# The end of a layer norm by TensorE, split first casts, and four order tables in a two-layer decoder trunk

## The chip, the cores and the metric

The kernel runs on one core of a Trainium2 chip. The metric is the device time of one execution in microseconds. Three runs of the kernel before took 552.74, 552.90 and 553.92 us; the median is 552.90.

## The reference

A trunk of two layers works on 256 tokens of width 1024. Each layer has a token mixer, a cross-attention into 256 memory tokens and a SwiGLU feed-forward block of width 2816. The residual is scaled by ALPHA and followed by a layer norm:

```python
x = layer_norm(ALPHA * x + sub, ln_mix_g[i], ln_mix_b[i])
x = layer_norm(ALPHA * x + swiglu(x, w_ffn_in[i], w_ffn_out[i]), ln_ffn_g[i], ln_ffn_b[i])
```

The mixer of layer 0 is a gated spatial mixer: u, v and the memory queries come from one projection of x, v is normalised and mixed over the positions of a 128-token chunk, and the result is multiplied by u. The mixer of layer 1 is causal attention with 12 heads. Everything is float32. What leaves the kernel is the layer norm behind the second feed-forward block: for each row, (r - mean) * g * rs + b, where rs is the reciprocal square root of variance plus epsilon.

## The kernel before

**Precision.** A float32 operand is kept as two parts that TensorE multiplies at its fast float32 rate: a high part, a rounded copy made by ScalarE (`nc.scalar.copy` in `split`, L379), and a low part, the difference, made by VectorE (L380). A product of two such operands takes three passes: high by high, low by high and high by low. Operands that aren't split (float32 on both sides) are multiplied as true float32, which the trace shows as two matmul instructions for each product.

**Weights.** All weights lie in one array in the order of use and are loaded in units of 128 x 2048 through a ring of four buffers (`Stream`, L194 to L290). SyncE's queue (SP) issues most loads, GpSimd's queue (POOL) those that are added onto a block already loaded (L220).

**The first projection.** L426 to L448 project x onto v. The contraction of 1024 runs in eight steps of 128 rows, kk from 0 to 7. A step's load brings 256 columns of x transposed, followed by 768 columns of weights. Step 0 comes in three pieces (x; 384 weight columns by ScalarE's queue; 384 more), the others in one. The step's x is split into `xT` (L439, L440), its weights into `hl`, in two cuts of 384 for steps 0 and 1. Twelve products follow (L446): for each half h of the weight columns, high by high, x low by weight high, x high by weight low, for both 128-token tiles. Ahead of them, 37 small bfloat16 products (L415) keep TensorE busy until the first load has landed.

**The u projections.** They follow (L943 to L953) as six tiles of PSUM, written by 16 products each. Each tile is read out by ScalarE (L950) and VectorE (L951). They share four PSUM buffers, tag "mm", with the two query tiles ahead of them, which L475 to L477 read out.

**The end.** Tokens are two tiles of 128 rows, 0 and 1. `last_tile` (L892 to L905) closes tile 1 in three column pieces of 512, 384 and 128. For each piece TensorE makes 18 products, VectorE adds them to the residual (L903) and takes statistics (L499). `finish` (L502 to L514) then aggregates the statistics (L505), adds epsilon (L507), lets GpSimd raise the sum to the power -0.5 (L508, called the power below), and for the same three pieces subtracts the mean and multiplies by the gain (L511, the subtract), multiplies by rs and adds the bias (L512, the scale), and stores (L514): two pieces by SP, the last by ScalarE's queue.

**The order of the work.** TensorE's instructions run as the program writes them. For VectorE, ScalarE and SP the order is written out in tables: `VECTOR_ORDER`, `SCALAR_ORDER` and `SYNC_ORDER` list the engine's instructions, numbered as the program issues them, in the order in which they are to run, and `keep_order` (L358) binds each to the one ahead of it. An engine works strictly along its table, so an instruction that waits holds all that stand behind it. GpSimd's order is left to the scheduler.

Of the kernel before, what the change touches and what calls it, by code (L numbers as in the profile page):

```python
# [30 lines left out]
LAST_PIECES = ((0, 512), (512, 896), (896, 1024))  # L31
PASSES = ((0, 0), (0, 1), (1, 0))
# [161 lines left out]
class Stream:  # L194
# [128 lines left out]
)  # L323
SCALAR_ORDER = (
# [42 lines left out]
def build(nc, tc, ins, out):  # L367
    ET = mybir.EngineType
    with (
# [15 lines left out]
        def mm_tile(name):  # L385
            return ps.tile([P, 512], F32, tag="mm", name=name)
# [836 lines left out]
```

## Time and profile before

| What | Value |
|---|---|
| Runs, median (lowest to highest) | 552.90 us (552.74 to 553.92) |
| Profiled execution, its own time | 552.48 us |
| Its span, first to last instruction | 550.8 us |
| TensorE matmul busy | 542.6 us, 99% |
| VectorE busy | 501.5 us, 91% |
| ScalarE busy | 374.5 us, 68% |
| GpSimd busy | 47.7 us, 9% |
| First product of the projection | 5.31 us |
| Last product's result taken up | 543.85 us |
| Mean granted TensorE clock | 0.996 |

Rows of a timeline give the start, the duration, the engine, the line, the operation, the tile written and the tiles read, the shape and the count of instructions merged; in brackets stands the idle time ahead and what ended it. Rows of a table by stretches give, for each engine (PE, weight loads, VectorE, ScalarE, GpSimd), the busy time and the number of instructions, then the granted clock, the share of the 16 DMA engines and GB/s. PE is TensorE, DVE VectorE, ACT ScalarE, POOL GpSimd; a q behind a name is that engine's queue. Rows of groups give the count, the busy time and the mean ns of one. Rows of the chain of waits give start, length and the work.

### The profile page before, as it was taken

How to read it: one execution, taken by the hardware profiler on the slowest of the kernel's cores; microseconds unless marked ns; L12 is line 12 of the kernel's file. 1: busy time of each engine (PE TensorE's matmuls, PEld its weight loads, DVE VectorE, ACT ScalarE, POOL GpSimd, SP SyncE). 2: the span in 40 equal slices, each digit the busy share in tenths (PEclk: the TensorE clock that was granted, in tenths of full speed). 3: DMA queues.
4: the chain of work that ended last, by engine and by line, in shares of the span. 5: the costliest groups of instructions: out<-in, count | busy, mean ns of one | idle time of the engine just before them, and what ended most of it. 6: DMA issues, size and time to landing. Idle time of an engine off the chain costs nothing.

```text
span 550.8 us, 7698 instructions
## 1 busy us (share of the span) xinstructions
PE 542.6 (99%) x2835; PEld 460.6 (84%) x2835; DVE 501.5 (91%) x707; ACT 374.5 (68%) x574; POOL 47.7 (9%) x59
## 2 busy tenths in 40 slices
PE   9999999999999999999999999999999999999994
PEld 8988878888888888888898888788888888888884
DVE  5799978999999999999989688589999999999997
ACT  5868759785858677683565667668768676876720
POOL 1012001020202020100000000111202020201000
PEclk9999999999999999999999999999999999999998
DMA  8997668479796988878539234513597698897622
GB/s 303 384 398 265 223 259 221 154 131 328 155 343 132 300 220 229 275 271 273 198 137 397 105 130 161 114 77 153 97 360 133 249 266 271 233 255 220 218 69 77
DMA packets 23718, 120.97 MB, mean 220 GB/s; under 512 B 2688, under 2 KB 4736, under 8 KB 13824
## 3 DMA queue, kind: packets, MB, share of 16 engines
q1 hardware_dynamic: 17344, 99.16, 47.8%
q0 software_dynamic: 5760, 20.97, 21.4%
q8 instruction: 22, 0.36, 0.3%
q10 hardware_dynamic: 576, 0.34, 0.3%
q14 instruction: 16, 0.13, 0.1%
HBM read 119.42 MB, written 1.05 MB: 219 GB/s over the span
## 4 chain that ended last, share of the span: by engine, by line
PE 98%; DMA 1%; DVE 1%; DVEq 0%; ACT 0%; issue 0%
PE fof L404 11%; PE Xf L404 10%; PE Xg L404 10%; PE fog L404 9%; PE Zg L404 7%; PE Zf L404 7%; PE qk L404 6%; PE opc L404 4%; PE opa L404 4%; PE va L404 3%; PE bv L404 3%; PE pu L404 3%; PE pvm L404 3%; PE hkm L404 2%; PE hqm L404 2%; PE pg L404 2%
## 5 line engine op out<-in xcount | busy, mean ns | idle before, releaser
L379 ACT CAST spl_s_M<-raw_s_T 128x1024 fp32r<-128x1024 f32 x80 | 82.4, 1052 | 22.9 <-DVE raw_s_T L259 18.0
L380 DVE TENSOR_TENSOR spl_s_M<-raw_s_T,spl_s_M 128x1024 fp32r<-128x1024 f32 x80 | 95.6, 1217 | 2.4 <-ACT spl_s_M L379 2.1
L380 DVE TENSOR_TENSOR spl_s_M<-raw_s,spl_s_M 128x1024 fp32r<-128x1024 f32 x60 | 71.7, 1217 | 3.2 <-ACT spl_s_M L379 3.1
L379 ACT CAST spl_s_M<-raw_s 128x1024 fp32r<-128x1024 f32 x60 | 61.0, 1050 | 17.5 <-DMA raw_s<-in_w 13.3
L404 PE MATMUL fof<-spl_w,htf 128*128 128x512 f32 x264 | 63.0, 390 | 0.0
L404 PEld LDWEIGHTS fof<-spl_w,htf 128*128 128x128 f32 x264 | 49.3, 188 | 10.2
L404 PE MATMUL fog<-spl_w,htg 128*128 128x512 f32 x228 | 54.2, 390 | 0.0
L380 DVE TENSOR_TENSOR spl_w<-raw_w,spl_w 128x1024 fp32r<-128x1024 f32 x44 | 53.2, 1215 | 0.1
L404 PEld LDWEIGHTS fog<-spl_w,htg 128*128 128x128 f32 x228 | 42.7, 188 | 8.8
L259 DVE TENSOR_TENSOR raw_s_T<-raw_s_T,raw_s 128x1024 f32<-128x1024 f32 x40 | 48.4, 1217 | 0.1
L379 ACT CAST spl_w<-raw_w 128x1024 fp32r<-128x1024 f32 x44 | 45.7, 1055 | 1.0 <-PE fof L404 1.0
L404 PE MATMUL qk<-x2T,spl_qk 128*128 128x512 f32 x192 | 36.0, 343 | 0.0
L220 POOL DMA_DIRECT2D raw_s<-in_w x20 | 17.1, 856 | 217.1 <-DVE spl_s_M L380 201.4
L404 PEld LDWEIGHTS qk<-x2T,spl_qk 128*128 128x128 f32 x192 | 29.4, 188 | 4.4
L404 PE MATMUL Xg<-spl_s_M,SgM 128*128 128x512 f32 x120 | 29.4, 394 | 0.0
L404 PE MATMUL Xf<-spl_s_M,SfM 128*128 128x512 f32 x120 | 29.3, 393 | 0.0
L404 PE MATMUL Zg<-spl_s_M,SgM 128*128 128x512 f32 x120 | 28.9, 390 | 0.0
L404 PE MATMUL Xf<-spl_s_M,x1T 128*128 128x512 f32 x120 | 28.9, 390 | 0.0
L404 PE MATMUL Zf<-spl_s_M,SfM 128*128 128x512 f32 x120 | 28.8, 389 | 0.0
L404 PE MATMUL Xg<-spl_s_M,x3T 128*128 128x512 f32 x120 | 28.8, 389 | 0.0
L404 PEld LDWEIGHTS Zg<-spl_s_M,SgM 128*128 128x128 f32 x120 | 22.5, 188 | 4.8 <-DVE SgM L380 0.2
L404 PEld LDWEIGHTS Xg<-spl_s_M,x3T 128*128 128x128 f32 x120 | 22.5, 188 | 4.7
(265 smaller groups left out, 1068.8 us busy)
## 6 DMA issues: line engine op xcount, KB each, us to landing
raw_w<-in_w SPq DMA_DIRECT2D x22, 1024.0 KB, 6.6
raw_s<-in_w SPq DMA_DIRECT2D x20, 1024.0 KB, 7.1
raw_s_T<-in_w SPq DMA_DIRECT2D x10, 1024.0 KB, 7.0
raw_s_T<-in_w POOLq DMA_DIRECT2D x20, 512.0 KB, 8.6
raw_s<-in_w POOLq DMA_DIRECT2D x20, 512.0 KB, 5.5
raw_o<-in_w SPq DMA_DIRECT2D x8, 1024.0 KB, 6.4
raw_qk<-in_w SPq DMA_DIRECT2D x6, 1024.0 KB, 4.8
raw_v<-in_w SPq DMA_DIRECT2D x7, 512.0 KB, 8.1
```

Source lines behind the costliest of these rows:

```text
L220: self.nc.gpsimd.dma_start(self.raw[name][:, sl], self.unit_ap(other)[:, sl], accum_op=ALU.add)
L259: self.nc.vector.tensor_add(raw, raw, self.raw[used[1]][:, sl])
L379: nc.scalar.copy(hi, src)
L380: nc.vector.tensor_sub(lo, src, hi.bitcast(F32))
L404: nc.tensor.matmul(o, lhsT, rhs, start=start, stop=stop, skip_group_check=on)
```

## The change

- Both tiles are finished and stored in pieces of 512, 256 and 256 columns. The products of `last_tile` keep their three pieces.
- For tile 1, columns 768 to 1023 are scaled by TensorE. A PSUM tile first receives the identity times the bias, two true float32 products that need nothing of the statistics. ScalarE multiplies the identity by rs, which gives a diagonal matrix; TensorE adds the diagonal times the subtracted columns; ScalarE copies the sum to SBUF and its queue stores it. VectorE only makes the subtract of that piece.
- The first 384 weight columns of step 0 are cast by two engines, 192 columns by ScalarE and 192 by VectorE. Step 1's load is cut in two: x with 384 weight columns, and the other 384.
- All order tables are new, and `POOL_ORDER` is added. In the new `VECTOR_ORDER`, 2 and 3 are the cast and the low part of step 0's x, 4 the new copy of 192 columns, 5 and 6 the low parts of its two weight cuts, 7 the cast of step 1's x; 26 to 29 read out the two query tiles, 36 and 37 are the adds of L951 for the first two u tiles; 660 to 667 finish tile 0, 668 to 675 are tile 1's adds and statistics, 676 to 682 finish tile 1. In the new `SYNC_ORDER`, 2 and 3 are the two loads of step 1, 6 and 7 those of steps 4 and 5. In the new `SCALAR_ORDER`, 10 to 13 are the casts of steps 4 and 5, x ahead of weights; 535 is tile 0's last store, 536 the diagonal, 537 the copy, 538 the last store.

```diff
+STORE_PIECES = ((0, 512), (512, 768), (768, 1024))
...
 VECTOR_ORDER = (
-    0, 2, 3, 4, 5, 6, 7, 8, 9, 10, 11, 12, 13, 14, 16, 15, 18, 17, 19, 20, 22, 21, 23, 24, 34, 29, 33, 25, 32, 38, 37,
...
-    661, 666, 663, 670, 664, 662, 671, 672, 673, 674, 675, 681, 676, 679, 677, 682, 680, 678,
+    0, 2, 4, 3, 5, 7, 6, 8, 9, 10, 11, 12, 13, 15, 14, 16, 17, 19, 18, 20, 22, 21, 24, 23, 1, 25, 34, 35, 30, 32, 38,
+    39, 33, 26, 47, 27, 56, 46, 49, 42, 43, 31, 48, 28, 57, 60, 37, 50, 36, 62, 29, 58, 51, 59, 40, 96, 61, 64, 41,
...
+    648, 633, 650, 646, 634, 649, 652, 651, 643, 653, 640, 647, 654, 669, 656, 658, 657, 655, 660, 659, 662, 668, 661,
+    664, 666, 670, 665, 663, 671, 672, 673, 667, 674, 675, 676, 677, 678, 682, 679, 680, 681,
 )
 SCALAR_ORDER = (
-    2, 3, 4, 5, 6, 7, 8, 9, 11, 10, 13, 14, 12, 15, 16, 0, 17, 1, 18, 19, 26, 27, 22, 24, 25, 31, 20, 32, 23, 41, 21,
...
+    2, 3, 4, 5, 6, 7, 9, 8, 0, 12, 10, 11, 13, 16, 15, 14, 17, 1, 18, 19, 26, 41, 22, 27, 24, 25, 31, 32, 42, 20, 23,
...
+    522, 530, 531, 523, 527, 532, 533, 534, 536, 535, 537, 538,
+)
+POOL_ORDER = (
+    0, 1, 5, 4, 6, 7, 2, 10, 3, 8, 9, 11, 12, 14, 13, 15, 16, 17, 18, 19, 20, 22, 21, 23, 24, 25, 26, 27, 28, 29, 30,
+    34, 33, 31, 32, 35, 36, 37, 38, 39, 40, 42, 41, 43, 44, 45, 46, 47, 48, 49, 50, 51, 52, 53, 54,
 )
 SYNC_ORDER = (
-    0, 1, 2, 3, 4, 18, 5, 6, 7, 8, 10, 9, 11, 12, 13, 14, 15, 19, 20, 16, 17, 24, 22, 25, 21, 26, 27, 28, 29, 23, 31,
...
+    0, 1, 3, 2, 4, 5, 19, 7, 6, 9, 8, 10, 11, 12, 20, 13, 14, 21, 15, 22, 16, 18, 23, 17, 25, 24, 26, 27, 28, 29, 30,
...
-    mine = [i for i in nc.cur_bb.bb.instructions if i.engine == engine and not str(i.opcode).startswith("Tile")]
+    mine = [i for i in nc.cur_bb.bb.instructions if i.engine == engine and not str(i.opcode).startswith(("Tile", "RegisterMove"))]
...
-                if kk == 0:
-                    for q, c0, c1 in ((nc.sync, 0, T), (nc.scalar, T, T + 384), (nc.sync, T + 384, D)):
-                        q.dma_start(rk[:, c0:c1], src[:, c0:c1])
-                else:
-                    nc.sync.dma_start(rk, src)
+                loads = {0: ((nc.sync, 0, T), (nc.scalar, T, T + 384), (nc.sync, T + 384, D)),
+                         1: ((nc.sync, 0, T + 384), (nc.sync, T + 384, D))}.get(kk, ((nc.sync, 0, D),))
+                for q, c0, c1 in loads:
+                    q.dma_start(rk[:, c0:c1], src[:, c0:c1])
...
                 for c0, c1 in cuts:
+                    if kk == 0 and c0 == 0:
+                        nc.scalar.copy(hl[:, 0, :192], rk[:, T:T + 192])
+                        nc.vector.tensor_copy(hl[:, 0, 192:c1], rk[:, T + 192:T + c1])
+                        nc.vector.tensor_sub(hl[:, 1, :c1], rk[:, T:T + c1], hl[:, 0, :c1].bitcast(F32))
+                        continue
                     split(hl[:, 0, c0:c1], hl[:, 1, c0:c1], rk[:, T + c0:T + c1])
...
-                for i, (c0, c1) in enumerate(LAST_PIECES if store else PIECES):
+                o = None
+                if store and tt:
+                    o = mm_tile("end")[:, :256]
+                    nc.tensor.matmul(o, ident, gb[:, 1, 768:], start=True, stop=False)
+                for c0, c1 in (STORE_PIECES if store else PIECES):
                     sl = slice(c0, c1)
                     nc.vector.scalar_tensor_tensor(r[:, sl], r[:, sl], mv[:, 0:1], gb[:, 0, sl], ALU.subtract, ALU.mult)
-                    nc.vector.scalar_tensor_tensor(r[:, sl], r[:, sl], rs, gb[:, 1, sl], ALU.mult, ALU.add)
+                    if c0 == 768 and o is not None:
+                        diag = const.tile([P, P], F32, name="diag")
+                        nc.scalar.mul(diag, ident, rs)
+                        nc.tensor.matmul(o, diag, r[:, sl], start=False, stop=True)
+                        nc.scalar.copy(r[:, sl], o)
+                    else:
+                        nc.vector.scalar_tensor_tensor(r[:, sl], r[:, sl], rs, gb[:, 1, sl], ALU.mult, ALU.add)
                     if store:
-                        (nc.scalar if i == len(LAST_PIECES) - 1 else nc.sync).dma_start(out[tt * P:(tt + 1) * P, sl], r[:, sl])
+                        (nc.scalar if c0 == 768 else nc.sync).dma_start(out[tt * P:(tt + 1) * P, sl], r[:, sl])
...
+    keep_order(nc, tc, ET.Pool, POOL_ORDER)
```

103 rows, old and new, of tables (SCALAR_ORDER, SYNC_ORDER, VECTOR_ORDER) are left out of this document.

## The prediction

> **What bounds the kernel now.** I read the page's busy line and chain of waits first, then the table by stretches, then the timelines of both ends.
>
> ```profile
> PE 542.6 (99%) x2835; PEld 460.6 (84%) x2835; DVE 501.5 (91%) x707; ACT 374.5 (68%) x574; POOL 47.7 (9%) x59
> PE 98%; DMA 1%; DVE 1%; DVEq 0%; ACT 0%; issue 0%
> ```
>
> ```profile
> 5.31:22.83 17.52, 17.52 (x97) 17.52 (x98) 13.08 (x21) 12.64 (x19) 0.00 (x0) 1.00 1.02 403
> 22.83:543.85 521.02, 520.98 (x2703) 439.25 (x2701) 483.74 (x674) 359.97 (x554) 45.38 (x50) 1.00 0.69 216
> 543.85:550.80 6.95, 0.00 (x0) 0.00 (x0) 3.88 (x10) 0.00 (x0) 0.85 (x1) 0.65 0.27 99
> ```
>
> From 5.31 to 543.85 TensorE (first busy column) is never without work: 17.52 of 17.52, then 520.98 of 521.02 us. So the middle, where most of the new order tables lie, can give nothing; it can only lose, where a reordered VectorE or ScalarE operand comes too late. Gains can come only from the 5.31 us ahead of the first product and the 6.95 us behind the last. A delay inside the stretch is paid in full. The profiled execution took 552.48 us, 1.68 beyond its span; the median of the runs, 552.90, is 0.42 above it. My sum is a difference made on this execution; I add it to the median.
>
> **The start: first casts.** Steps are the eight 128-row slices kk of the first projection, counted from 0, with 12 products each. The view is the timeline of VectorE and ScalarE.
>
> ```profile
> 4.52 0.29 DVE L439 CAST x0T<-raw_v 128x256 fp32r<-128x256 f32 x1 [3.52 <-DMA raw_v<-in_w]
> 5.29 1.07 DVE L380 TENSOR_TENSOR spl_v<-raw_v,spl_v 128x384 fp32r<-128x384 f32 x2
> 7.17 0.29 DVE L439 CAST x0T<-raw_v 128x256 fp32r<-128x256 f32 x1 [0.80 <-DMA raw_v<-in_w]
> 4.75 1.03 ACT L379 CAST spl_v<-raw_v 128x384 fp32r<-128x384 f32 x2 [2.21 <-DMA raw_v<-in_w]
> 9.78 0.41 ACT L439 CAST x0T<-raw_v 128x256 fp32r<-128x256 f32 x1 [0.48 <-DMA raw_v<-in_w]
> 10.09 0.83 ACT L379 CAST spl_v<-raw_v 128x768 fp32r<-128x768 f32 x1
> 10.95 0.96 DVE L380 TENSOR_TENSOR spl_v<-raw_v,spl_v 128x768 fp32r<-128x768 f32 x1 [0.23 <-ACT spl_v L379]
> 13.22 0.84 ACT L379 CAST spl_v<-raw_v 128x768 fp32r<-128x768 f32 x1 [0.16 <-DMA raw_v<-in_w]
> ```
>
> The first product waits for ScalarE's 384-column cast (4.75 plus half of 1.03). At 0.41 for 256 columns and 0.51 for 384, 192 columns take about 0.35 (bounds 0.26, half, and 0.41), so it ends at 5.10. VectorE's own 192 columns fit behind its 0.29 us cast, from 4.75 to about 5.05. The product starts at 5.15, 0.16 earlier. The clock is worth a look here:
>
> ```profile
> 6.64:545.95 539.31, 537.17 (x2795) 455.44 (x2794) 497.76 (x699) 372.15 (x571) 46.06 (x51) 1.00 0.70 221
> 545.95:550.80 4.85, 0.00 (x0) 0.00 (x0) 1.88 (x4) 0.00 (x0) 0.17 (x1) 0.50 0.29 108
> ```
>
> ```profile
> 5.31 1.01 PE L404 MATMUL va<-spl_v,x0T 128*128 128x384 f32 x2
> 7.94 0.51 PE L404 MATMUL va<-spl_v,x0T 128*128 128x384 f32 x2
> 14.18 0.51 PE L404 MATMUL va<-spl_v,x0T 128*128 128x384 f32 x2
> ```
>
> Products 12 and 48 of this stage start at 7.94 and 14.18, so one takes 0.173 us. The first two take 1.01 where a later pair takes 0.51: half speed. The trace's record of the granted clock begins, at 1.00, at 6.64. So work that moves ahead of 6.64 runs at half speed, and 0.16 us earlier is 0.08 to 0.16 gained; I take 0.10.
>
> That gain meets two places of the new order. **First**, VECTOR_ORDER now has "7, 6": the cast of step 1's x (7) ahead of step 0's second low part (6). The cast waits for step 1's load, here until 7.17, and the new loads put that piece last (SYNC_ORDER "3, 2"), so it lands no sooner with the same bytes ahead. Instruction 6, one half of the 1.07 us pair (0.55), would run from about 7.38 to 7.93. Queued behind it for TensorE is product 11, due at 7.76 before and 7.66 now; it starts at 7.98, and I add 0.08 for the restart (an estimate: half of the 0.16 by which a pair's 0.51 exceeds two times 0.173). TensorE is then 0.30 behind. **Second**, step 5 is loaded ahead of step 4 ("7, 6" in SYNC_ORDER), so step 4 lands where step 5 did, 13.22. ScalarE then needs 0.31 to its next start and 0.83, and VectorE another 0.96: the low part is there at 15.37. Product 53, the first to use it, was due at 15.04 (14.18 plus five times 0.173). TensorE is at least 0.36 behind. The two don't add: the later the stream is, the less the second costs. I take +0.36 (bounds -0.16, if step 1's piece lands by 6.8 and step 4 by 12.8, and +0.45). The extra load instruction costs SP 0.43 us; it is hidden, as the 16 engines are full in this stretch (share 1.02); uncovered it would cost those 0.43.
>
> GpSimd's table and the table of ScalarE move casts, loads and masks by places; POOL is 9% busy and I cost it at nothing, its cover being the other 91%; if that were gone, an accumulating load would be late by the power or mask put ahead of it, 0.4 to 1.4 us.
>
> **The end.** Again the row first, then the new order.
>
> ```profile
> 544.77 0.35 DVE L511 SCALAR_TENSOR_TENSOR xres<-xres,mvg,gb1ffn 128x128 f32<-128x128 f32 x1
> 545.04 0.15 DVE L507 TENSOR_SCALAR rsg<-mvg 128x1 f32<-128x1 f32 x1
> 545.11 1.27 DVE L511 SCALAR_TENSOR_TENSOR xres<-xres,mvg,gb1ffn 128x384 f32<-128x384 f32 x2
> 545.27 0.85 POOL L508 TENSOR_TENSOR rsg<-rsg,mhalf 128x1 f32<-128x1 f32 x1 [7.93 <-DVE rsg L507]
> 547.86 0.33 SPq L514 DMA_DIRECT2D out<-xres  x1
> ```
>
> The DMA issues of that stretch give KB each and us to landing:
>
> ```profile
> out<-xres SPq DMA_DIRECT2D x2, 256.0 KB, 2.2
> out<-xres SPq DMA_DIRECT2D x2, 192.0 KB, 1.9
> out<-xres ACTq DMA_DIRECT2D x2, 64.0 KB, 1.6
> ```
>
> The end is the last store: issued at 547.86, landed 2.0 later (its own share of the 2.2 median), at 549.87, and 0.93 more to the span's end. The new VectorE order is: epsilon directly behind the aggregate, then the 512-column subtract, the 256-column subtract (768 on), the 512-column scale, then subtract and scale of 512:768. Epsilon starts at 544.77, 0.27 earlier, and the power would start at 545.00. But the power takes as long as the VectorE instruction under way lets it: 0.56 us beside a 0.41 one, 1.42 beside a 1.23 one, each ending about 0.4 behind it:
>
> ```profile
> 91.03 0.41 DVE L470 TENSOR_TENSOR kkm<-hkm,kkm 128x256 fp32r<-128x256 f32 x1
> 91.21 0.56 POOL L522 TENSOR_TENSOR rsa<-rsa,mhalf 128x1 f32<-128x1 f32 x1 [3.93 <-DVE rsa L521]
> 363.57 1.23 DVE L380 TENSOR_TENSOR spl_s_M<-raw_s,spl_s_M 128x1024 fp32r<-128x1024 f32 x1
> 363.80 1.42 POOL L522 TENSOR_TENSOR rsc<-rsc,mhalf 128x1 f32<-128x1 f32 x1 [17.45 <-DVE rsc L521]
> ```
>
> Beside the 0.74 us subtract, from 544.84 to 545.58, it ends at 545.99, not at 545.56; before it ended at 546.12. So 0.27 earlier yields 0.13. VectorE's scale of 512 runs 546.02 to 546.77, the 256-column subtract (0.48, between 0.35 and 0.61) to 547.16, its scale from 547.20 to 547.68, the store is issued at 547.71. 128 KB should land in 1.75 (between 1.6 and 1.9): 549.46.
>
> The last quarter goes another way. ScalarE's diagonal waits for the power; behind it on ScalarE stand the first tile's last store, the copy and the last store. TensorE has only the second product behind that wait, VectorE's scale the last two instructions and both SP stores. Prices:
>
> ```profile
> L576 ACT ACTIVATE pb<-pb,mb 128x128 f32<-128x128 f32 x12 | 4.7, 395 | 6.5 <-DVE mb L567 6.5
> L950 ACT COPY uT<-pu 128x256 f32<-128x256 f32 x6 | 2.2, 369 | 2.3 <-PE pu L404 2.3
> 70.74 1.88 PE pvm L404 x16
> ```
>
> Diagonal 0.40 (0.30 to 0.47): 546.04 to 546.44. The product has true float32 operands; the nearest row has eight such products of 256 columns on half the array in 1.88 us, so 0.47 on all of it (bounds half of that and, at half clock, twice). Weights and the way until the result is out take 0.35, an estimate from the pair above (0.16 behind the second product, and about as much ahead): it ends at 547.31; copy until 547.71; store issued 547.74, landed 549.49. The bias product with the identity runs in TensorE's empty time at 543.8 and delays nobody. So the end is 549.49, 0.38 earlier. At half clock weights, product and copy end at 548.29, the store lands at 550.07: 0.20 later than before.
>
> Which clock? The record falls to 0.50 at 545.95, 2.1 us behind the last product. The identity product moves that by 0.43, and the diagonal's weights load at 546.49. As a fixed delay behind the last product that is even; but the identity product also fills the stretch ahead of the fall, 1.70 of 3.41 busy in place of 1.27 (second row below), so I take full speed, at two to one.
>
> ```profile
> 3.23:6.64 3.41, 3.29 (x23) 3.02 (x21) 1.79 (x4) 1.02 (x2) 0.00 (x0) 1.00 0.98 342
> 542.54:545.95 3.41, 1.27 (x12) 1.13 (x11) 3.15 (x10) 0.00 (x0) 0.68 (x1) 1.00 0.36 137
> ```
>
> The Trainium skill, page "TensorE: Matmul & The Clock Gate", section "Part 1: The HAM clock gate", has the clock decided by a window of 3.41 us that runs freely of the kernel. The trace agrees: rise and fall lie 539.31 apart, 158 windows of 3.413, the window before the rise was 3.29 busy and that before the fall 1.27. By that rule the phase differs between executions, and the diagonal runs fast in some and slow in others; the sum would be the two ends above by turns.
>
> One instruction is moved onto the path: the first tile's last scale (667) now stands ahead of the last tile's final add. Its cover is an idle stretch that the new order fills with the first tile's subtracts:
>
> ```profile
> 538.75 0.69 DVE L903 TENSOR_TENSOR xres<-xres,last 128x512 f32<-128x512 f32 x1 [0.67 <-PE last L404]
> ```
>
> I cost it at nothing; uncovered, 0.2 to 0.4.
>
> Sum: +0.36 - 0.38 = -0.02. Forecast 552.9.
>
> **Rivals.**
> - The start doesn't stall (-0.10), end as above: -0.48, 552.4. For it: a wait ends with a load's last part, and in another execution that may come 0.5 sooner; against it: both loads were waited for here (0.80 and 0.16 idle).
> - The diagonal meets the half clock: +0.36 + 0.20 = +0.56, 553.5.
> - Slower: a TensorE buffer in the u projections. Six tiles of 2.77 us each run from 28.38; the fourth (36.69) needs a PSUM tile that VectorE has read.
>
> ```profile
> 28.38 16.64 PE pu L404 x96
> 30.54 0.40 DVE L477 SCALAR_TENSOR_TENSOR qqm<-hqm,qqm 128x256 fp32r<-128x256 f32 x1
> ```
>
> Before, the second q tile was read out at 30.54. Now that read (29) stands behind two u splits, three memT splits, a km split and a 1.00 us normalisation; laying the rows behind one another in the new order (an estimate), the first buffer to come free is that of add 37, at 36.8. Each further 1.23 us split (the row at 363.57) that comes late there delays TensorE by as much, beyond the 0.36 that it is late anyway. From 1.1 us of such waiting on it decides: one split more gives 554.1, two 555.4. For it: VectorE is 91% busy; against it: the rows leave it just in time.
> - Faster: the first product catches a full clock at once. The half-clock stretch (5.31 to 6.64) is worth 0.67 at most: -1.15, 551.7.
>
> **How the numbers follow.** Chances: forecast 0.42, no stall 0.20, half clock 0.20, buffer 0.13, clock at the start 0.05. From the bounds: best start and end -0.16 - 0.5 (the end with the store of 64 KB's 1.6), so 552.2; worst +0.45 with the slow end, +0.20, and 667 uncovered, +0.3, so 553.9. That range leaves out the buffer and the early clock, 0.18. About 0.2% (1.1 us) is what a measurement of this kernel can tell from no change: faster 0.05 (the early clock), same 0.80, slower 0.15 (the buffer, and 0.02 for several bounds at once).
>
> **What would show it.** VectorE's low part of step 0 starting behind a cast near 7.2, with TensorE idle before product 11; a TensorE wait near 15; the power ending near 546.0 plus the stream's delay; the fp32 product with the diagonal taking 0.5 or 0.9. TensorE idle between 23 and 540 would make the forecast wrong, as would a first tile's last scale that holds the final add.

## The result and the profile after

The changed kernel takes 557.12 us (median of 8 runs, 555.79 to 560.07); the kernel before, beside it, 552.82 (552.27 to 553.92). The ratio is 1.0078, 95% interval 1.0064 to 1.0092: 4.3 us slower. The forecast was 552.9, the range 552.2 to 553.9. The spread has grown from 1.7 to 4.3 us, which is a finding of its own. The profiled execution took 556.10, 1.0 below the median, so its trace holds only 3.6 of the 4.3.

The first fence shows the busy line and the chain's shares, on the page of the changed kernel.

```profile
PE 544.5 (98%) x2839; PEld 459.8 (83%) x2839; DVE 501.7 (90%) x707; ACT 375.2 (68%) x576; POOL 48.0 (9%) x59
PE 81%; DVE 7%; issue 5%; DMA 4%; ACT 2%; POOL 1%; SPq 0%; POOLq 0%; ACTq 0%; DVEq 0%
```

Before, the chain was TensorE for 98%. Now 19% of it runs through other engines and loads: TensorE waits somewhere in the middle. The table by stretches says where. Columns: length, then busy time of TensorE, weight loads, VectorE, ScalarE, GpSimd, then clock, DMA share and GB/s. The first three rows are start, middle and end; the last three cut the middle into the first feed-forward block, the second layer's attention, and the second block.

```profile
5.04:22.70 17.66, 17.44 (x97) 16.81 (x98) 14.07 (x24) 13.52 (x21) 0.00 (x0) 1.00 1.03 401
22.70:547.04 524.34, 521.99 (x2704) 439.20 (x2703) 483.19 (x671) 359.23 (x552) 46.30 (x52) 1.00 0.68 214
547.04:554.40 7.36, 1.53 (x4) 0.42 (x3) 3.65 (x9) 0.77 (x2) 0.99 (x1) 0.69 0.25 90
76.00:270.00 194.00, 192.44 (x899) 160.16 (x897) 184.87 (x209) 137.29 (x182) 21.12 (x25) 1.00 0.76 228
270.00:400.00 130.00, 129.21 (x780) 110.61 (x779) 108.20 (x229) 89.36 (x185) 7.77 (x9) 1.00 0.47 154
400.00:547.00 147.00, 147.00 (x683) 122.79 (x682) 142.36 (x155) 94.37 (x115) 13.08 (x16) 1.00 0.73 218
```

Middle: 524.34 where it was 521.02, so +3.32 (idle time shows 2.35 of it; the ends of matmuls are modelled, and part of a wait is counted as busy). End: 7.36 where it was 6.95. The first projection ends 0.13 earlier, at 22.70, in an execution whose clock rose early (at 3.72; at 6.64 in the profile before). The largest stall lies in the first feed-forward block. The timeline around it:

```profile
139.87 1.05 ACT L384 CAST spl_s_M<-raw_s_T 128x1024 fp32r<-128x1024 f32 x1 [1.88 <-DMA raw_s_T<-in_w]
140.36 0.27 PE L849 MATMUL tpf<-ident,m1f 128*128 128x128 f32 x1
140.82 0.59 ACT L827 ACTIVATE sgf<-Xf 128x512 f32<-128x512 f32 x1
141.44 0.69 DVE L828 SCALAR_TENSOR_TENSOR m5f<-m5f,sgf 128x512 f32<-128x512 f32 x1 [2.02 <-ACT sgf L827]
142.19 0.33 PE L849 MATMUL tpf<-ident,m5f 128*128 128x128 f32 x1 [1.56 <-DVE m5f L828]
```

Read it upwards. TensorE waits for m5f, VectorE for sgf, and ScalarE stood at a cast that waited 1.88 for a load. In SCALAR_ORDER that cast (161) now stands ahead of sgf (149); before it stood behind. Two waits in the second layer's attention follow the same pattern, on the timeline of TensorE:

```profile
340.05 2.23 PE L409 MATMUL qk<-x2T,spl_qk 128*128 128x512 f32 x11 [0.24 <-ACT pT L1089]
...
354.65 1.20 PE L1087 MATMUL pt<-ident,pb 128*128 128x128 f32 x9 [0.40 <-DVE pb L601]
```

From start to start, beyond what such neighbours need elsewhere, the four largest stalls cost 1.73 (at 140), 0.41 (340), 0.57 (354) and 0.31 (385): 3.0 of the 3.32.

The end, on the timeline of the changed kernel:

```profile
547.97 0.15 DVE L516 TENSOR_SCALAR rsg<-mvg 128x1 f32<-128x1 f32 x1
548.20 0.99 POOL L517 TENSOR_TENSOR rsg<-rsg,mhalf 128x1 f32<-128x1 f32 x1 [5.71 <-DVE rsg L516]
549.22 0.40 ACT L527 ACTIVATE diag<-ident,rsg 128x128 f32<-128x128 f32 x1 [10.19 <-POOL rsg L517]
549.67 1.08 PE L528 MATMUL end<-xres,diag 128*128 128x256 f32 x2 [2.18 <-ACT diag L527]
550.79 0.37 ACT L529 COPY xres<-end 128x256 f32<-128x256 f32 x1 [1.17 <-PE end L528]
551.20 0.35 ACTq L533 DMA_DIRECT2D out<-xres  x1
```

Counted from the last tile's last add (547.04; 543.85 before), the power ends at 2.15 where 2.14 was predicted, the diagonal at 2.58 (2.59). The products take 1.08, and ScalarE's store, the last, is issued 4.16 after the add, where 3.89 was predicted.

That late store does not set the end here. SP's last store, issued 3.87 after the add, landed 6.00 after it. SP then goes through the signals of the other DMAs (their semaphores) one by one, 0.06 apart, from 6.03 to 6.46, and ScalarE's store landed at 6.34, while that went on. So SP waits for stores only once in this profile (total, times, longest):

```profile
SPq L1239 <- DMA out<-xres: 1.7, 1, 1.7
```

### The profile page after: what moved, and what is told of

The parts are those of the page before. It is cut to its first block, busy times and chain, and to the rows that moved or that the text cites. A ratio compares the mean times of both kernels' runs of the same rounds, so it can differ in the third digit from the quotient of the medians.

```text
span 554.4 us, 7706 instructions
## 1 busy us (share of the span) xinstructions
PE 544.5 (98%) x2839; PEld 459.8 (83%) x2839; DVE 501.7 (90%) x707; ACT 375.2 (68%) x576; POOL 48.0 (9%) x59
## 4 chain that ended last, share of the span: by engine, by line
PE 81%; DVE 7%; issue 5%; DMA 4%; ACT 2%; POOL 1%; SPq 0%; POOLq 0%; ACTq 0%; DVEq 0%
PE fof L409 10%; PE Xg L409 9%; PE fog L409 9%; PE Xf L409 7%; PE Zg L409 7%; PE qk L409 6%; PE Zf L409 5%; PE opa L409 4%; PE bv L409 3%; PE pu L409 3%; PE va L409 3%; DMA raw_s_T<-in_w 3%; PE hqm L409 2%; DVE spl_s_M L385 2%; PE pvm L409 2%
## 5 line engine op out<-in xcount | busy, mean ns | idle before, releaser
L409 PEld LDWEIGHTS Zf<-spl_s_M,SfM 128*128 128x128 f32 x120 | 22.5, 188 | 4.7
```

What stands on the lines that cost most here:

```text
L409: nc.tensor.matmul(o, lhsT, rhs, start=start, stop=stop, skip_group_check=on)
```

## Experiments

All runs are medians beside the kernel before on the same chip; the kernel before was 552.65 to 552.91 throughout. "Old order" means the entries of the kernel before, renumbered.

### The middle, one pair, GpSimd's table, the end alone

First run: the middle of three tables in the old order, GpSimd's table gone.

```diff
 VECTOR_ORDER = (
...
-    1, 25, 34, 35, 30, 32, 38, 39, 33, 26, 47, 27, 56, 46, 49, 42, 43, 31, 48, 28,
+    25, 35, 30, 34, 26, 33, 39, 38, 31, 28, 32, 29, 42, 47, 36, 27, 46, 50, 56, 43,
...
 SCALAR_ORDER = (
...
-    26, 41, 22, 27, 24, 25, 31, 32, 42, 20, 23, 43, 44, 36, 37, 28, 45, 21, 29, 46,
+    26, 27, 22, 24, 25, 31, 20, 32, 23, 41, 21, 36, 42, 28, 37, 45, 43, 29, 46, 49,
...
-    keep_order(nc, tc, ET.Pool, POOL_ORDER)
```

> The changed kernel with the middle of the three order tables as in the kernel before (renumbered): VectorE's entries from place 24 to the last 28, ScalarE's from 20 to the last 12, SP's from 14 to the last 12. Start, end and their entries stay as changed; GpSimd has no table. If the new order in the middle costs the time (theory M), TensorE has no stall between 23 and 540, and the time falls by the 3.3 us that the stretch between the first projection and the last product became longer: 553.2 to 554.2. If start and end cost it (theory E, end +0.4 in the profile and the rest in what a profile does not show), it stays at 556 to 558.

554.41 us, ratio 1.0028 (1.0018 to 1.0038), 0.2 above the band that theory M gave. TensorE waits nowhere between 23 and 540; only 30 products at 528, where old and new order meet, take 7.28 in place of 6.96. The new order in the middle costs 2.7 us (557.12 - 554.41; 2.5 if each is first taken against the kernel before beside it); 1.8 over the kernel before (552.65) are left for start and end.

Second run: one pair of ScalarE's table.

```diff
-    159, 161, 149, 162,
+    159, 149, 161, 162,
```

> The changed kernel with one pair of ScalarE's table exchanged: 161, 149 becomes 149, 161, so the SiLU that writes sgf runs ahead of the cast of raw_s_T that waits for a load. Theory S (the 1.73 us TensorE stall at 140 is that pair alone): no stall at 140, time 555.2 to 555.6 with the median at 557.1 now, and less spread, since the stall ends with a DMA. Theory P (the loads are late because of GpSimd's table, and something else then waits for them): the stall moves on to a later instruction, and the time falls by less than 0.6.

557.28 us, 1.0084 (1.0065 to 1.0104): nothing gained, theory S falls. The stall at 140 is gone, but others stand at 162 and 192 in the profiled execution, the slowest of the six (560.07). The timeline at 162:

```profile
160.57 1.05 ACT L385 CAST spl_s_M<-raw_s_T 128x1024 fp32r<-128x1024 f32 x1 [4.00 <-DMA raw_s_T<-in_w]
161.65 2.36 DVE L386 TENSOR_TENSOR spl_s_M<-raw_s_T,spl_s_M 128x1024 fp32r<-128x1024 f32 x2 [2.98 <-ACT spl_s_M L385]
163.93 1.22 DVE L386 TENSOR_TENSOR spl_w<-raw_w,spl_w 128x1024 fp32r<-128x1024 f32 x1
165.20 0.98 PE L410 MATMUL fof<-spl_w,htf 128*128 128x512 f32 x3 [2.58 <-DVE spl_w L386]
```

The pattern is the same with other instructions: VectorE stands at two splits whose load is late, and the split that TensorE needs now is queued behind them. The load is an accumulating one of GpSimd's. Its row among the DMA issues (KB, us to landing), first of the changed kernel's profile, then of this run:

```profile
raw_s_T<-in_w POOLq DMA_DIRECT2D x1, 512.0 KB, 6.5
```

```profile
raw_s_T<-in_w POOLq DMA_DIRECT2D x1, 512.0 KB, 10.4
```

It was issued at 150.1 both times and landed 3.9 later here. As these traces have it, the stall's place is a matter of which load is late in an execution. That would widen the spread as well.

Third run: GpSimd's order left to the scheduler.

```diff
-    keep_order(nc, tc, ET.Pool, POOL_ORDER)
```

> The changed kernel without GpSimd's table; nothing else differs. Theory P (the accumulating load that was issued at 91.49 behind a power, 5.08 later than before, makes what follows late): the stall at 140 goes, and the time falls by 1.7 or more, to 555.4 or less. Theory S: the load is not what the cast at 139.87 waits for, the stall stays, and the time is 557 within 0.6.

558.65 us, 1.0097 (1.0080 to 1.0114): 1.5 longer, not shorter. In this form theory P falls: on the new order the table is not what costs. That it helps is not shown, as the two intervals overlap. (The accumulating load that was 5 us late in the first profile went out early here, and TensorE stalled at 190 and 196.)

Fourth run: the change of the end alone, in the kernel before. Its diff is that of `finish` in the change, with the tables' last entries:

```diff
+                if store and tt:
+                    o = mm_tile("end")[:, :256]
+                    nc.tensor.matmul(o, ident, gb[:, 1, 768:], start=True, stop=False)
...
-    661, 666, 663, 670, 664, 662, 671, 672, 673, 674, 675, 681, 676, 679, 677, 682, 680, 678,
+    661, 667, 660, 663, 665, 669, 664, 662, 670, 671, 672, 666, 673, 674, 675, 676, 677, 681, 678, 679, 680,
```

> The kernel before with the change of the end alone: three store pieces of 512, 256 and 256, TensorE's scaling of the last 256 columns, and the last 28 entries of VectorE's, the last of ScalarE's and the last 12 of SP's table from the changed kernel. By the recorded sum -0.38, 552.4. By the trace of the changed kernel (from the last tile's add to the end 7.35 where it was 6.95) +0.40, 553.2: half clock in the products with the diagonal, and a last store that took 2.19 to land in place of 1.75.

553.00 us, 1.0007 (0.9998 to 1.0016): +0.35, which can't be told from no change; a gain of 0.38 (0.9993) lies outside the interval. Here the profile met the full clock. Its last rows, then its DMA issues:

```profile
547.08 0.70 PE L522 MATMUL end<-xres,diag 128*128 128x256 f32 x2 [2.18 <-ACT diag L521]
...
548.22 0.38 ACTq L527 DMA_DIRECT2D out<-xres  x1
```

```profile
out<-xres ACTq DMA_DIRECT2D x1, 128.0 KB, 2.1
out<-xres SPq DMA_DIRECT2D x1, 128.0 KB, 2.2
```

ScalarE's store is issued 3.77 after the add (544.45 here), where 3.89 was predicted; SP's goes last, at 3.87, where 3.86 was predicted. But 128 KB took 2.1 to 2.2 to land, not 1.75.

### The two blocks of the middle, and the start

The first feed-forward block in the old order, in three tables; GpSimd's table stays.

```diff
 VECTOR_ORDER = (
...
-    112, 142, 143, 129, 113, 144, 115, 116, 114, 146, 117, 124, 118, 119, 145, 126,
+    142, 112, 129, 144, 143, 145, 115, 116, 113, 114, 117, 146, 118, 124, 119, 149,
...
 SYNC_ORDER = (
...
-    37, 38, 40, 39, 41, 43,
+    37, 39, 38, 40, 41, 43,
```

> The changed kernel with the stretch of the first feed-forward block (about 80 to 270 us) ordered as before in VectorE's, ScalarE's and SP's tables (VectorE's places 115 to 325, ScalarE's 86 to 267, SP's 37 to 71); GpSimd's table and all else stay as changed. Theory L (the new order there puts casts and splits that wait for a load ahead of work that TensorE needs soon, and a late load stalls it at a place that differs by execution: 140, 162, 192, 189 and 196 so far): no stall between 80 and 270, the three of layer 1 (0.41, 0.57, 0.31) stay; 557.1 - 1.5 to 2.5 = 554.6 to 555.6, and the runs lie within 1.5 us of one another. Theory P (GpSimd's table makes the loads late): it still holds, so stalls stay, 556.5 or more.

559.14 us, 1.0120 (1.0103 to 1.0138): 2.0 longer. Theory L was wrong as it stood, and the run brought theory G of the next section: in the trace two accumulating loads are issued together at 122, one of them held.

Second, the second layer's attention in the old order.

```diff
 VECTOR_ORDER = (
...
-    320, 322, 321, 323, 336, 331, 337, 332, 342, 343, 365, 370, 399, 371, 364, 338,
+    322, 320, 321, 323, 331, 336, 337, 332, 342, 364, 343, 370, 371, 398, 399, 338,
...
 SCALAR_ORDER = (
...
-    260, 274, 269, 275, 270, 278, 279, 272, 290, 291, 298, 299, 312, 313, 276, 320,
+    274, 260, 269, 275, 270, 278, 279, 290, 291, 298, 272, 299, 312, 313, 276, 320,
```

> The changed kernel with the second layer's attention and the way into its feed-forward block (about 277 to 390 us) ordered as before in VectorE's, ScalarE's and SP's tables; all else as changed. The stalls at 340, 354 and 385 stand in three profiles with the same lengths (0.40, 0.57, 0.31), so they are of the order and not of a load: they go, 557.1 - 1.3 = 555.8, with the spread of the runs as wide as the changed kernel's. If they are only the echo of an earlier delay, the time stays at 557.

555.96 us, 1.0064 (1.0051 to 1.0076): 1.16 less, but the intervals overlap, so the time alone can't show a gain. The traces can: the stalls at 340, 354 and 385 are gone here and in every profile with the old order in that stretch, and they stand in all six with the new one. They were of the order. The stalls of the first block (here at 141 and 189) stay. A wait of 1.0 at 280, where the two orders meet, is new, and TensorE is 1.4 later behind it, about what the three had cost (1.3); so the profiled execution is hardly shorter than that of the changed kernel (555.96 against 556.10).

Third and fourth: the start alone in the kernel before, with the new entries, and with the old ones.

```diff
+                    if kk == 0 and c0 == 0:
+                        nc.scalar.copy(hl[:, 0, :192], rk[:, T:T + 192])
...
-    0, 2, 3, 4, 5, 6, 7, 8, 9, 10, 11, 12, 13, 14, 16, 15,
+    0, 2, 4, 3, 5, 7, 6, 8, 9, 10, 11, 12, 13, 15, 14, 16,
```

> The kernel before with the change of the start alone: the first casts split over two engines, step 1's load in two, and the first 24 entries of VectorE's, 20 of ScalarE's and 14 of SP's table from the changed kernel. By the recorded sum +0.36: 553.0 to 553.2. In the profile: VectorE's second low part of step 0 behind the cast of step 1's x, and TensorE idle for 0.3 to 0.5 ahead of product 11. If the first product's 0.1 to 0.5 earlier start carries through: 552.3.

```diff
-    0, 2, 4, 3, 5, 7, 6, 8, 9, 10, 11, 12, 13, 15, 14, 16,
+    0, 2, 4, 3, 5, 6, 7, 8, 9, 10, 11, 12, 13, 14, 15, 17,
```

> As the run with the start alone, but the orders of the start stay as before: VectorE takes both low parts of step 0 ahead of step 1's cast, SP loads step 1's first piece ahead of its second and step 4 ahead of step 5. If the two orderings are what the start costs, it is 0.36 to 0.5 below the run with the new order: 552.3 to 552.6, 0 to 0.4 below the kernel before. If the split itself costs or gives nothing, 552.7.

554.04 us, 1.0026 (1.0017 to 1.0036), against 552.90, 1.0007 (0.9998 to 1.0016). The start as changed costs 1.34, over three times the 0.36 of the sum; in the old order it costs next to nothing and gains nothing. The timeline of the run with the start alone:

```profile
9.48 0.83 ACT L382 CAST spl_v<-raw_v 128x768 fp32r<-128x768 f32 x1 [2.15 <-DMA raw_v<-in_w]
...
10.36 0.96 PE L407 MATMUL va<-spl_v,x0T 128*128 128x384 f32 x4 [0.43 <-ACT spl_v L382]
```

TensorE catches up with the loads: ScalarE's cast of step 2's weights starts at 9.48 in this execution, at 8.46 in that of the profile before. The predicted wait near 15 is there too (0.3, for the cast of step 4's weights). Some 0.4 of the 1.34 lies at the other end of the kernel (the run with one more load, below).

### GpSimd's table, and one more load

The old middle again (554.41), now with GpSimd's table; and the same with one pair of that table exchanged.

```diff
+    keep_order(nc, tc, ET.Pool, POOL_ORDER)
```

> The changed kernel with the middle of VectorE's, ScalarE's and SP's tables as before (the run that took 554.41), and GpSimd's table kept. That table has 14 ahead of 13: the accumulating load that VectorE's old order frees first stands behind the one freed later. Theory G (the table has to fit VectorE's order): loads issued at about 116 and 121 go out together at 122, TensorE stalls by 2 to 4 us near 136 to 146, time 557 to 558.5. Theory N (GpSimd is idle enough for any order, as the prediction had it): 554.4 within 0.6.

```diff
-    0, 1, 5, 4, 6, 7, 2, 10, 3, 8, 9, 11, 12, 14, 13, 15, 16, 17, 18, 19, 20, 22, 21, 23, 24, 25, 26, 27, 28, 29, 30,
+    0, 1, 5, 4, 6, 7, 2, 10, 3, 8, 9, 11, 12, 13, 14, 15, 16, 17, 18, 19, 20, 22, 21, 23, 24, 25, 26, 27, 28, 29, 30,
```

> The run with the old middle and GpSimd's table (557.76), with one pair of that table exchanged: 14, 13 becomes 13, 14, the order in which VectorE's old order frees the two halves. Theory G1 (that pair alone costs the 3.35 between 557.76 and 554.41): the two loads go out near 116 and 121, no stall at 136 to 146, 554.4 within 0.6. Theory G2 (the mask or the power ahead of the first accumulating load, or the pair 10 ahead of 9, matter as well): 555.5 or more.

557.76 us, 1.0098 (1.0082 to 1.0113), and 554.75, 1.0032 (1.0022 to 1.0043). The table costs 3.35, and 3.0 of that are the pair 14, 13. GpSimd's timeline, first with the pair as in the table, then exchanged:

```profile
114.25 0.86 POOL L221 DMA_DIRECT2D raw_s<-in_w  x1 [1.42 <-DVE spl_s_M L388]
120.41 1.73 POOL L221 DMA_DIRECT2D raw_s_T<-in_w  x2 [5.30 <-ACT m5f L791]
```

```profile
115.11 0.86 POOL L221 DMA_DIRECT2D raw_s<-in_w  x1 [1.42 <-DVE spl_s_M L388]
116.85 0.84 POOL L221 DMA_DIRECT2D raw_s_T<-in_w  x1 [0.88 <-DVE spl_s_M L388]
121.27 0.86 POOL L221 DMA_DIRECT2D raw_s_T<-in_w  x1 [3.58 <-DVE spl_s_M L388]
```

GpSimd is idle for 5.30 with a load in its table whose tile is free: 13 waits behind 14, and goes out 4 us late. TensorE pays from 135 to 144; this is its longest wait:

```profile
137.29 3.02 PE L412 MATMUL Xf<-spl_s_M,x1T 128*128 128x512 f32 x12 [2.26 <-DVE m5f L827]
```

The stretch 76 to 270 in the same order of runs:

```profile
76.00:270.00 194.00, 190.80 (x885) 158.37 (x884) 183.96 (x207) 135.47 (x179) 20.18 (x25) 1.00 0.76 229
```

```profile
76.00:270.00 194.00, 194.00 (x906) 161.80 (x906) 187.79 (x212) 137.55 (x182) 20.15 (x25) 1.00 0.77 231
```

With that, once more: the first block in the old order, without GpSimd's table.

```diff
-    keep_order(nc, tc, ET.Pool, POOL_ORDER)
```

> The run with the first feed-forward block ordered as before (559.14), now without GpSimd's table. Theory G (the stalls at 136 and 145 of that run, 3.4 us, came from GpSimd's table): they go, 555 to 556, with the three stalls of layer 1 (1.3) and perhaps one in the second feed-forward block left. If the stretch ahead of 80, which is as changed, hands the block its delay: stalls between 100 and 200 stay, 558 or more.

555.05 us, 1.0041 (1.0028 to 1.0053), all runs within 0.9; TensorE is busy for all of 76 to 270. Theory G holds. Against the changed kernel the first block's new order, GpSimd's matching table included, costs 2.1; without that table 3.6 (558.65 - 555.05).

Two runs on the end of the kernel. One more load in the kernel before; and the split start in the old order with one load fewer.

```diff
-IN_HALVES = ("qm0", "u0", "km0")
+IN_HALVES = ("qm0", "u0", "km0", "o1_3")
```

> The kernel before with a single change: the last weights of layer 1's output projection are loaded in two halves in place of one, one more entry in SP's table. TensorE needs them 20 us later, so no work is late. Theory C (one more load shifts which semaphore the last store takes; SP then looks at it second of ten and spends 0.06 us on each of the others after it has landed): the last store lands as before, but 1.33 in place of 0.90 lie between that and the end, and the time is 0.4 longer, 553.1. Otherwise 552.7.

```diff
-IN_HALVES = ("qm0", "u0", "km0")
+IN_HALVES = ("qm0", "u0")
```

> The run with the split start in the old order (552.90), with one load fewer elsewhere: the first memory-key weights, needed 11 us after they land, come in one load in place of two, so the number of loads is that of the kernel before. Theory C: the end takes 0.90 after the last landing again, and the time is 552.4 to 552.5, 0.2 to 0.3 below before. If the 0.2 that the start cost lies in the start itself: 552.9.

553.29 us, 1.0010 (1.0001 to 1.0018), and 552.94, 1.0003 (0.9994 to 1.0012). The first is +0.38, as theory C has it; its trace has 1.33 between the last landing and the end, where the kernel before has 0.90. SP's waits for stores (total, times, longest), of the kernel before and then of this run:

```profile
SPq L1219 <- DMA out<-xres: 1.1, 2, 0.7
```

```profile
SPq L1219 <- DMA out<-xres: 1.6, 1, 1.6
```

Before, SP waits for one store, then for the last; here its one wait is already for the last store, and seven more checks, 0.06 apart, come after it. The second run is inconclusive: its trace has the 0.90 again, but the 0.04 by which the time differs from that of `start_clean` is nothing that can be told.

### Which order does it

SP's old order in the middle, all else as changed.

```diff
 SYNC_ORDER = (
...
-    20, 13, 14, 21, 15, 22, 16, 18, 23, 17, 25, 24, 26, 27, 28, 29, 30,
+    13, 14, 15, 16, 20, 21, 17, 18, 25, 23, 26, 22, 27, 28, 29, 30, 24,
```

> The changed kernel with the middle of SP's table as before (places 14 to the last 12); VectorE's, ScalarE's and GpSimd's tables as changed. Theory Y (SP's new order, with weights of later steps loaded ahead of ones needed sooner, makes the loads late): the stalls between 80 and 270 go, 555 to 555.6. Theory V (VectorE's order decides when a buffer is freed, SP only follows): 557.1 within 0.8.

576.93 us, 1.0437 (1.0413 to 1.0460), far from both theories. VectorE's timeline, then TensorE's:

```profile
44.17 0.69 DVE L388 TENSOR_TENSOR memT<-mraw,memT 128x512 fp32r<-128x512 f32 x1 [9.81 <-ACT memT L387]
...
48.96 0.37 DVE L973 TENSOR_TENSOR uT<-uT,pu 128x256 f32<-128x256 f32 x1
```

```profile
49.39 1.01 PE L412 MATMUL pu<-x0T,spl_u 128*128 128x512 f32 x2 [11.03 <-DVE uT L973]
```

It is the prediction's slower rival, at its place: VectorE's new order has the memory splits ahead of the reads that free a PSUM tile, SP's old order loads the memory late, and TensorE stands in the u projections for 11 us. The rest of the 20 us was not taken apart.

Last, the start's two orders one by one, each on the split start that took 552.90.

```diff
-    0, 2, 4, 3, 5, 6, 7, 8, 9, 10, 11, 12, 13, 14, 15, 17, 16, 19, 18, 20, 21, 23, 22, 24,
+    0, 2, 4, 3, 5, 7, 6, 8, 9, 10, 11, 12, 13, 15, 14, 16, 17, 19, 18, 20, 22, 21, 24, 23,
```

> The run with the split start in the old order (552.90), with the first 24 entries of VectorE's table from the changed kernel, so that the cast of step 1's x stands ahead of step 0's second low part. By the recorded step named First: TensorE waits ahead of product 11, and the time is 0.2 to 0.3 longer, 553.1 to 553.2. If it is SP's order that costs the 1.1 between 554.04 and 552.90: 552.9.

```diff
-    0, 1, 2, 3, 4, 5, 19, 6, 7, 8, 9, 11, 10, 12,
+    0, 1, 3, 2, 4, 5, 19, 7, 6, 9, 8, 10, 11, 12,
```

> The run with the split start in the old order (552.90), with the first 14 entries of SP's table from the changed kernel: step 1's second piece ahead of its first, step 5 ahead of step 4. By the recorded step named Second: 0.1 to 0.4 longer, 553.0 to 553.3. If nearly all of the 1.1 between 554.04 and 552.90 is SP's order: 553.7 to 554.1.

555.08 us, 1.0038 (1.0025 to 1.0052), and 554.62, 1.0029 (1.0020 to 1.0038): over the 552.90, 2.2 and 1.7. Alone, neither costs less than both together with ScalarE's entries (1.14), as far as the overlapping intervals tell. In the first, VectorE takes 24 (the first query weights' low part) ahead of 23 (step 7's):

```profile
20.43 1.23 DVE L383 TENSOR_TENSOR spl_qm<-raw_qm,spl_qm 128x1024 fp32r<-128x1024 f32 x1 [2.89 <-ACT spl_qm L382]
...
21.58 0.95 DVE L383 TENSOR_TENSOR spl_v<-raw_v,spl_v 128x768 fp32r<-128x768 f32 x1
...
22.58 1.66 PE L407 MATMUL va<-spl_v,x0T 128*128 128x384 f32 x8 [1.53 <-DVE spl_v L383]
```

In the profile of the run with all three new tables of the start there is no such wait. So the tables are one schedule: what an entry costs can't be read from its own table.

## Why the prediction was wrong, by its steps

**The middle, and GpSimd's table: the step that failed.** The prediction said rightly that the middle "can give nothing; it can only lose", and then costed it at nothing: GpSimd's table, "its cover being the other 91%", and the new middle through one rival at one place. The middle measured +2.7 (557.12 - 554.41). The first feed-forward block alone measured 2.1. The three stalls of the second layer's attention are 1.3 in the trace, 1.2 by a time that noise could explain. Idle time is no cover for an order: an idle engine with a fixed order waits at its head. On the old order the table cost 3.35 at 9% busy. The bound of 0.4 to 1.4 took the power or the mask as what goes ahead; what went ahead was another load, which waited itself. In the changed kernel taking the table out gains nothing (558.65); there the cost is that of the new order as a whole.

**The slower rival** (0.13) had the mechanism, VectorE at an instruction that is not ready with TensorE's need queued behind, but the wrong place. In the changed kernel the u projections don't stall; with SP's old order they do, for 11 us.

**The start, +0.36.** Both named places are in the traces. First, in the changed kernel:

```profile
6.49 0.29 DVE L443 CAST x0T<-raw_v 128x256 fp32r<-128x256 f32 x1 [0.80 <-DMA raw_v<-in_w]
6.70 0.55 DVE L385 TENSOR_TENSOR spl_v<-raw_v,spl_v 128x384 fp32r<-128x384 f32 x1
7.30 1.14 PE L409 MATMUL va<-spl_v,x0T 128*128 128x384 f32 x5 [0.22 <-DVE spl_v L385]
8.00 0.84 ACT L384 CAST spl_v<-raw_v 128x768 fp32r<-128x768 f32 x1 [0.58 <-DMA raw_v<-in_w]
```

Cast 7 waits 0.80 for the load, low part 6 follows, and product 11 waits for it (7.30). Second is the wait near 15, in the run with the start alone (the prediction's own 15.37 and 15.04 lie 0.33 apart, not 0.36). The term was mis-sized: 1.34 alone. Some 0.4 of that is the end's checks, a step that the sum did not have. By the traces the rest goes with a load that the sum took to come as before, that of step 2, in a stretch that keeps the 16 DMA engines busy (share 1.03). In the eleven profiles with the changed start, ScalarE's cast of step 2's weights (8.00 in the last row) starts anywhere from 7.93 to 9.80, and the products that follow the projection start 14.50 to 14.59 after that cast in every one. In the three profiles with the old start the cast starts at 8.41 to 8.59. Why the load comes so unevenly is open. The earlier first product bought nothing that lasts: the split in the old order gained nothing. Nor does a clock that has risen before the first product, the rival with 0.05: it had in four of the eleven, and in three of these the projection ends 1.1 to 1.6 later than in the profile before.

**The end, -0.38.** The order of events was right: power and diagonal within 0.01, the last store of full clock at 3.87 (3.86 and 3.89 for the two were predicted). The half clock reached the products in 5 of the 11 profiles that have the new end (last store issued 4.16 to 4.29 after the add, 3.87 in the others), so the rival with 0.20 was nearly a coin; but it cost nothing. From the last add to the last instruction these five take 7.07 to 7.35, and the five with the same loads at full clock 7.33 to 7.58; it was 6.92 in the profile before.

Two things failed. One is the landing: 1.75 for 128 KB, read off between 1.6 for 64 KB and 1.9 for 192. The last two stores, 128 KB each, took 1.86 to 2.35 in these eleven, as long as one of 256 KB (2.0). The other is what comes behind it: 0.93 in the prediction, 1.35 from the landing of SP's store in the changed kernel's profile, because the extra load moved that store's check ahead of seven others. With the new end and no extra load it stayed at 0.90, and the whole end took 6.97. The Trainium skill, page "DMA: Bandwidth & Descriptors", section "Anatomy of one DMA", has a constant of some 2 us that is mostly completion, for DMAs that GpSimd issues; these stores by SP and ScalarE are near it at 128 and 256 KB, while the 1.6 of the 64 KB store lies under it.

**The account.** Measured alone: start 1.34, end 0.35, first block 2.1, second attention 1.2: 5.0 for the 4.3 that all cost together. Each has an interval of 0.5 to 0.8 us to either side, so this settles no more than the rough sizes.

**Left open.** Which entries of the first block's new order cost the 2.1 is not settled: exchanging the pair behind one stall moved the stall and not the time. In three profiles with the new order there, the second block has waits too (the longest 1.2, 0.7 and 0.4); they were not pursued. That late loads set the place is read from traces; making the loads lighter was not tried.

## What to carry to other kernels

A table of order is a promise about when loads land. Before costing a reordered stretch at nothing, look at each instruction that moved ahead of others, ask what it waits for, and take the latest landing seen in several profiles, not in one; an idle engine is no cover, since its head can wait. Tables of several engines that were made together stand or fall together, so an undone part measures the mismatch as well. Before adding a load or a store, see which wait the end looks at last.

## What the runs showed of the hardware

- One more load cost about 0.4 us at the end (553.29 against 552.91, interval 0.01 to 0.18%). SP checks the landings' signals in a fixed order, 0.06 us a check, and seven checks that it had finished before the last landing now come behind it: 1.33 us from there to the end in place of 0.90.
- The same accumulating load of 512 KB took 6.5 and 10.4 us from issue to landing in two executions, issued at the same time.
- A long stall costs clock as well. The granted clock in the run with SP's old order:

```profile
38.30:40.73 2.43, 0.06 (x1) 0.00 (x0) 0.00 (x0) 0.00 (x0) 0.00 (x0) 1.00 1.01 416
40.73:49.39 8.66, 0.00 (x1) 0.01 (x1) 4.97 (x10) 5.87 (x9) 0.37 (x1) 0.50 0.24 59
49.39:54.38 4.99, 4.99 (x15) 4.31 (x16) 4.99 (x6) 0.57 (x2) 2.49 (x2) 0.50 0.44 184
```

It fell 2.4 after TensorE ran dry, and came back 4.99 after TensorE had work again; the two changes lie 13.65 apart, four windows of 3.41. That is the free-running window of the Trainium skill's page "TensorE: Matmul & The Clock Gate", section "Part 1: The HAM clock gate".
